# A hand-fixed TensorE order in the experts' stage, and the crowded-expert loop ahead of the first pair

## The chip, the cores and the metric

The kernel runs on one core of a Trainium2 chip. The metric is the device time of one execution in microseconds (us), as the median of several runs. A core has five engines that run their own instruction streams: TensorE (PE in the profile; its weight loads are PEld), VectorE (DVE), ScalarE (ACT), GpSimd (POOL) and SyncE (SP), which here does nothing but issue DMA transfers. They wait for each other by semaphores.

## What is computed

Two model blocks on 256 tokens of width 1024, all in fp32. The change lies in the mixture of experts that ends the first block. The router gives every token two of 32 experts; only the chosen pairs need to be computed:

```python
def hier_moe(h, w_rg, b_rg, w_re, b_re, w_eg, w_eu, w_ed):
    ...
    eid = g_idx * EXP_PER_GROUP + top_i
    gates = jnp.sum(jax.nn.one_hot(eid, N_EXPERTS, dtype=jnp.float32) * (pg_sel * pw)[..., None], axis=1)
    out = jnp.zeros_like(t)
    for e in range(N_EXPERTS):
        hid = jax.nn.silu(t @ w_eg[e]) * (t @ w_eu[e])
        out = out + gates[:, e:e + 1] * (hid @ w_ed[e])
    return out.reshape(bsz, s, d)
```

`w_eg` and `w_eu` are 1024x512 for each expert, `w_ed` is 512x1024. The second block (two hybrid layers) follows; it starts with a norm of the sum of the first block's stream and the experts' output.

## The kernel before

**Places and pairs.** Each expert gets 64 places. Two experts form a pair, so that a pair fills 128 partitions of PSUM, and there are 16 pairs `i`. A product of one expert has 64 weight columns (`z` = 0 or 1, the expert in the pair) and writes the upper or the lower 64 partitions. In the trace an fp32 product is two records: TensorE goes over its data twice.

**The steps of a pair.**
- `gather`: for two pairs at a time, the tokens are picked into their places by products with a 0/1 matrix `sel` (made by VectorE in `select`). The rows stand split in two parts, `h2h` and `h2l`. There are four PSUM banks, `k` = 0, 2, 4, 6; VectorE (k = 0, 4) and ScalarE (k = 2, 6) copy them to `XT`, which has one buffer.
- `front` with `w_eg` (result `pg`), then `front` with `w_eu` (`pu`): 8 values of `k`, two experts, 16 products each.
- `hidden`: tanh on ScalarE, then two passes on VectorE give `hid`.
- `middle`: four transposes of `hid` (`turn`), two of `sel` (`places`), and the gate of each place (`pgs`, two tiny products); ScalarE copies the transposes to `hidT` and `selT`.
- `down`: 16 products with `w_ed`, result `ys` in two banks `n`.
- `scatter`: for each half `n`, `yh` (ScalarE) and `yl` (VectorE), then four products with `selT` into PSUM tiles `mx` (two buffers), which VectorE adds to `x`.

In iteration `i` the program writes `front(pg)`, `middle` of pair i-1, `scatter` of pair i-2, `front(pu)`, `hidden`, sometimes `gather`, and `down` of pair i-1. This is not the order on TensorE: a list scheduler orders each engine's instructions by its own costs and priorities.

**The weights.** They come in 192 loads of 1 MB (two halves for each of 96 matrices; two experts, so four loads for a `front` or a `down`) through one queue of SP, in the order of use (`expert_halves`, L923). The loads go round 18 slots: `wq` (8), `wp` (4) and `wr` (6). From load 162 on, `wp` is left out, since the next layer's weights go there, and 14 slots remain. SP issues a load when the slot's last reader on TensorE is done. Loads use eight semaphores in turn, so that a load also waits for the one eight before it.

**The crowded-expert loop.** `more_rounds` handles experts with more than 64 tokens: every engine reads `mxi` (L1091), the number of further rounds, and branches (L1092). With these inputs it is zero and the body is skipped. An engine that skips it still raises the semaphores which the body would have raised. It does so only when its own work ahead of the branch is done: TensorE's products for TensorE, and all eight load semaphores for SP. The loop stands behind the first pair's `down`.

Of the kernel before, what the change touches and what calls it, by code (L numbers as in the profile page):

```python
# [10 lines left out]
F32 = mybir.dt.float32  # L11
# [8 lines left out]
P = 128  # L20
S = 256
NT = S // P
# [70 lines left out]
class K:  # L93
# [837 lines left out]
    def moe(self, x, es, e0):  # L931
# [19 lines left out]

        def gather(sel, n, XT, first=False):

            def add(ps, k, j, t, hp, start, stop, **kw):
                return nc.tensor.matmul(ps[:, j, :n], hp[:, t, (k + j) * P:(k + j + 1) * P],
                                        sel[:, t].rearrange("p e s -> p (e s)"), start=start, stop=stop, **kw)

            banks = []
            if first:

                for ps, k in zip(self.accT() + self.accT(), range(0, 8, 2)):
                    banks.append(ps)
                    for hp in (h2h, h2l):
                        for j in range(2):
                            ins = add(ps, k, j, 0, hp, hp is h2h and j == 0, False, skip_group_check=True)
                            if hp is h2h and j == 0:
                                head = ins
                            elif hp is h2h:
                                tc.add_manual_dep(ins.ins, head.ins.name, mybir.DependencyInfo(
                                    mybir.DependencyClass.NoSync, mybir.DependencyReason.DATA))  # L970
            for k in range(0, 8, 2):
                ps = banks[k // 2] if first else self.mx.tile([P, 2, 256], F32, name="mx")
                for j in range(2):
                    if first:
                        for hp in (h2h, h2l):
                            add(ps, k, j, 1, hp, False, hp is h2l, skip_group_check=True)
                    else:
                        for i, (hp, t) in enumerate(((h2h, 0), (h2h, 1), (h2l, 0), (h2l, 1))):
                            add(ps, k, j, t, hp, i == 0, i == 3)
                if k % 4:  # L980
                    for j in range(2):
                        nc.scalar.activation(XT[:, k + j, :n], ps[:, j, :n], AF.Copy, scale=self.g2[:, k + j:k + j + 1])
                else:
                    nc.vector.tensor_tensor(XT[:, k:k + 2, :n], ps[:, :, :n],
                                            self.g2[:, k:k + 2].unsqueeze(2).to_broadcast([P, 2, n]), op=ALU.mult)

# [12 lines left out]
        def turn(hid, rows, f=""):  # L999
            hT = q.tile([P, 4, P], F32, name=f + "hidT", tag="XT" if f else "hidT", bufs=1)  # L1000
# [25 lines left out]
        def scatter(sT, py, rows, gs, po=None):  # L1026

            for n in range(2):
                yh, yl = parts(py, n, rows, gs)
                for t in range(NT):  # L1030
                    ps = po[t][n] if po else self.mx.tile([P, 512], F32, name="mx")
                    nc.tensor.matmul(ps, sT[:rows, t], yh[:rows], start=not po, stop=False)
                    nc.tensor.matmul(ps, sT[:rows, t], yl[:rows], start=False, stop=not po)
                    if not po:
                        xs = x[:, t, n * 512:(n + 1) * 512]
                        nc.vector.tensor_add(xs, xs, ps)
# [14 lines left out]

        def front(ps, XT, i):

            o = 2 * (i % 2)
            ww = self.experts()
            for k in range(8):
                for z in range(2):
                    nc.tensor.matmul(ps[64 * z:64 * z + 64], XT[:, k, 64 * (o + z):64 * (o + z + 1)], ww[z][k],  # L1058
                                     start=k == 0, stop=k == 7)
            self.expert_halves(4)  # L1060

        def middle(i, hid, sel):
# [5 lines left out]
            pgs = self.mx.tile([P, 512], F32, name="mx")  # L1068
# [8 lines left out]
        def down(hT):  # L1077
# [3 lines left out]
            for k, n in kn:  # L1081
                for z in range(2):
                    nc.tensor.matmul(py[n][64 * z:64 * z + 64], hT[:, k, 64 * z:64 * z + 64],  # L1083
                                     ww[z][k][:, n * 512:(n + 1) * 512], start=k == 0, stop=k == 3)
            self.expert_halves(4)
            return py

        def more_rounds():
# [3 lines left out]
            with tc.If(n > 0), tc.For_i(0, n, 1):  # L1092
                nc.vector.tensor_scalar(Rm, Rm, -64.0, None, op0=ALU.add)
                with tc.For_i(0, 32, 1) as e:
# [5 lines left out]
                    sel = select(Rc, 0, 1, q, "sel")  # L1100
                    XT = q.tile([P, 8, 64], F32, name="f_XT", tag="XT", bufs=1)
                    gather(sel, 64, XT)
# [20 lines left out]
                    scatter(places(sel[:, :, 0], 64, "f_"), py, 64, gs)  # L1123

        def group(g):

            sels[g] = select(R, 4 * g, 4, p if g % 2 else q, "sel")
            XT = q.tile([P, 8, S], F32, name="XT", bufs=1)
            gather(sels[g], 256, XT, g == 0)
            return XT  # L1130
# [18 lines left out]
        XT = group(0)  # L1149
        G, mxi = self.route_rest(p)  # L1150
        self.out("G", G)

        for i in range(16):
            pg, pu = self.accs(2, 0)
            front(pg, XT, i)
            if i and i != 2:
                mid[i - 1] = middle(i - 1, hid[i - 1], sels[(i - 1) // 2])
            if i > 1:
                scatter(mid[i - 2][1], ys[i - 2], P, mid[i - 2][2])
            front(pu, XT, i)  # L1160
            hid[i] = hidden(pg, pu, P)
            if i == 2 and "positions_2" in A:
                with tc.issue_after(self.hid_ins.ins):
                    self.rope_tables(q)
            if i == 12:
# [3 lines left out]
                for z, g in enumerate(gs2):  # L1169
                    nc.gpsimd.dma_start(self.grow[8 * z:8 * z + 8], g.rearrange("(a b) -> a b", a=8))  # L1170
            if i == 13:
                gsq = factors()
            if i == 1:
                ys[0] = down(mid[0][0])
                mid[1] = middle(1, hid[1], sels[0])
                if self.rounds:
                    more_rounds()
            if i % 2 and i < 15:
                XT = group(i // 2 + 1)
            if i > 1:  # L1180
                ys[i - 1] = down(mid[i - 1][0])
# [5 lines left out]
        scatter(mid[14][1], ys[14], P, mid[14][2], po)  # L1187
        with tc.high_priority(offset=5000):
            ys[15] = down(mid[15][0])
# [844 lines left out]
```

## Time and profile before

| | us |
|---|---|
| median of 3 runs (1845.67 to 1847.8) | 1845.88 |
| profiled execution | 1852.19 |
| its span, first to last instruction | 1850.4 |
| experts' products begin | 183.25 |
| last product of the experts' stage, start of what follows | 688.31 |

The experts' stage so takes 505 us of the span. TensorE is busy for 1771.3 us of the span (96%), VectorE for 977.8 (53%), ScalarE for 743.0 (40%), GpSimd for 117.1 (6%). In the page's 40 slices of 46.3 us each, the DMA rate is 386 and 289 GB/s in the slices from 185 to 278 us, 419 or 420 in the six slices after, then 290, 389 and 166. The page's busy TensorE includes modelled ends and pipelined matmuls, so 96% busy is not 96% at its peak.

### The profile page before, as it was taken

The numbers are of one execution on the slowest core, as the hardware profiler recorded it, in microseconds if no ns is written. First come the engines' busy times: TensorE is split into PE (matmuls) and PEld (weight loads), VectorE is DVE, ScalarE is ACT, GpSimd is POOL, SyncE is SP. The second block draws the span as 40 slices with busy tenths as digits, with TensorE's granted clock in tenths as the row PEclk, the third lists the DMA queues.
The fourth block names the chain that finished last, engine by engine and source line by source line (L and its number), as shares of the span: only waits on it lengthen the run. The fifth ranks groups of instructions, "written<-read, shape, count | busy, mean of one in ns | idle before, by whom it ended". The sixth has DMA issues, their size and how long they took to land. (4 is left out here: it accounts for less than half of the span.)

```text
span 1850.4 us, 27201 instructions
## 1 busy us (share of the span) xinstructions
PE 1771.3 (96%) x10929; PEld 1341.2 (72%) x10929; DVE 977.8 (53%) x1860; ACT 743.0 (40%) x1260; POOL 117.1 (6%) x159
## 2 busy tenths in 40 slices
PE   7999779999999998999999999999999999999998
PEld 6876334433333336879987999997879998999997
DVE  6666022212221227766467585557766567576555
ACT  3454011111111123556464454444555555555443
POOL 4101000000000003000002000002100001100000
PEclk8888989999999999999999999999999999999999
DMA  7456979999997946325644565654414744455552
GB/s 255 148 201 277 386 289 420 419 419 420 419 420 290 389 166 217 108 78 183 194 138 149 185 228 182 188 198 149 163 47 138 217 160 141 147 181 184 192 193 80
DMA packets 153465, 414.51 MB, mean 224 GB/s; under 512 B 13347, under 2 KB 42868, under 8 KB 128632
## 3 DMA queue, kind: packets, MB, share of 16 engines
q1 hardware_dynamic: 152408, 410.49, 62.0%
q0 software_dynamic: 784, 2.18, 0.3%
q8 instruction: 87, 1.43, 0.3%
q14 instruction: 42, 0.34, 0.1%
q10 hardware_dynamic: 144, 0.07, 0.0%
HBM read 411.63 MB, written 2.12 MB: 224 GB/s over the span
## 5 line engine op out<-in xcount | busy, mean ns | idle before, releaser
L170 DVE TENSOR_TENSOR wlo<-raw,whi 128x1024 fp32r<-128x1024 f32 (+4 forms) x372 | 440.2, 1184 | 306.4 <-ACT whi L169 305.7
L169 ACT CAST whi<-raw 128x1024 fp32r<-128x1024 f32 (+4 forms) x384 | 385.4, 1005 | 384.6 <-PE acc L231 155.2
L231 PE MATMUL acc<-xTl,whi 128*128 128x256 f32 x992 | 286.6, 291 | 1.0 <-DVE xTl L385 1.0
L231 PE MATMUL acc<-xTh,whi 128*128 128x256 f32 x992 | 286.7, 291 | 0.0
L231 PE MATMUL acc<-xTh,wlo 128*128 128x256 f32 x992 | 280.4, 290 | 0.0
L1058 PE MATMUL acc<-raw,XT 128*64 128x512 f32 x1024 | 253.0, 605 | 0.0
L231 PEld LDWEIGHTS acc<-xTh,whi 128*128 128x128 f32 x992 | 193.6, 195 | 6.5 <-issue 5.9
L231 PEld LDWEIGHTS acc<-xTl,whi 128*128 128x128 f32 x992 | 193.4, 195 | 6.6 <-issue 5.0
L231 PEld LDWEIGHTS acc<-xTh,wlo 128*128 128x128 f32 x992 | 190.0, 195 | 5.5 <-issue 5.2
L1058 PEld LDWEIGHTS acc<-raw,XT 128*64 128x64 f32 x1024 | 76.4, 139 | 146.9 <-issue 142.3
L1083 PE MATMUL acc<-raw,hidT 128*64 128x512 f32 x512 | 133.6, 597 | 0.0
L178 PE MATMUL acc<-wlo,xTh 128*128 128x512 f32 (+4 forms) x368 | 129.5, 352 | 0.0
L177 PE MATMUL acc<-whi,xTh 128*128 128x512 f32 (+4 forms) x368 | 129.4, 352 | 0.0
L179 PE MATMUL acc<-whi,xTl 128*128 128x512 f32 (+4 forms) x368 | 128.5, 349 | 0.0
L177 PE MATMUL acc<-whi,ffh 128*128 128x512 f32 x256 | 101.0, 394 | 0.0
L178 PE MATMUL acc<-wlo,ffh 128*128 128x512 f32 x256 | 100.7, 393 | 0.0
L179 PE MATMUL acc<-whi,ffl 128*128 128x512 f32 x256 | 100.7, 393 | 0.0
L1083 PEld LDWEIGHTS acc<-raw,hidT 128*64 128x64 f32 x512 | 43.9, 136 | 67.0 <-issue 64.4
L1022 DVE SCALAR_TENSOR_TENSOR yl<-acc,gs,yh 128x512 fp32r<-128x512 f32 x32 | 24.0, 749 | 113.0 <-ACT yh L1021 111.8
L178 PEld LDWEIGHTS acc<-wlo,xTh 128*128 128x128 f32 x368 | 69.6, 189 | 8.4 <-issue 2.2
L177 PEld LDWEIGHTS acc<-whi,xTh 128*128 128x128 f32 x368 | 69.6, 189 | 7.5 <-issue 1.2
L179 PEld LDWEIGHTS acc<-whi,xTl 128*128 128x128 f32 x368 | 69.4, 188 | 7.2 <-issue 1.2
(688 smaller groups left out, 3099.0 us busy)
## 6 DMA issues: line engine op xcount, KB each, us to landing
raw<-in_w_in SPq DMA_DIRECT2D x70, 1024.0 KB, 5.1
raw<-in_w_eg SPq DMA_DIRECT2D x64, 1024.0 KB, 16.6
raw<-in_w_eu SPq DMA_DIRECT2D x64, 1024.0 KB, 17.9
raw<-in_w_ed SPq DMA_DIRECT2D x64, 1024.0 KB, 13.8
raw<-in_w_ff SPq DMA_DIRECT2D x64, 1024.0 KB, 5.2
raw<-in_w_out SPq DMA_DIRECT2D x12, 1024.0 KB
raw<-in_w_branch SPq DMA_DIRECT2D x12, 1024.0 KB, 5.2
raw<-in_w_in SPq DMA_DIRECT2D x8, 792.0 KB
```

The source lines that it names most:

```text
L169: nc.scalar.copy(hi[:, :nk, :n], src)
L170: ins = (nc.gpsimd if pool else nc.vector).tensor_sub(lo[:, :nk, :n], src, hi[:, :nk, :n])
L177: mm(ps, ahi, bhi, start=start, stop=False)
L178: mm(ps, ahi, blo, start=False, stop=False)
L179: self.mm_ins = mm(ps, alo, bhi, start=False, stop=stop)
L231: ins = mm(ps[c // 2][:, c % 2, :], w[:, j, c * P:(c + 1) * P], x[:, kx + k + j, :], start=first and c % 2 == 0, stop=k + j == nk - 1 and ...
L1022: nc.vector.scalar_tensor_tensor(yl[:rows], py[n][:rows], gs, yh[:rows].bitcast(F32), op0=ALU.mult, op1=ALU.subtract)
L1058: nc.tensor.matmul(ps[64 * z:64 * z + 64], XT[:, k, 64 * (o + z):64 * (o + z + 1)], ww[z][k], start=k == 0, stop=k == 7)
L1083: nc.tensor.matmul(py[n][64 * z:64 * z + 64], hT[:, k, 64 * z:64 * z + 64], ww[z][k][:, n * 512:(n + 1) * 512], start=k == 0, stop=k == 3)
```

## The change

1. `manual_schedule` for TensorE: from the first iteration on, its instructions run in the order in which the program writes them. The other engines are scheduled as before.
2. The program writes them so that the products of the two experts with the same `k` (and `n`) always follow each other. `middle` of pair i-1 comes behind `k` = 1 of `front(pg)`, the scatter of half 0 behind `k` = 4, half 1 behind `k` = 0 of `front(pu)`. In odd iterations the banks of `gather` come behind `k` = 5 and 6 of `front(pu)` and behind the second and fourth step of `down`. `down` of pair i-1 comes after `hidden` in every iteration, also for i = 1.
3. `pgs` takes a `tp` tile in place of an `mx` tile. `tp` has two buffers and now gets three tiles in each `middle`.
4. `more_rounds` comes before the first pair. Its tiles have tags that fit there.

```diff
-        def scatter(sT, py, rows, gs, po=None):
+        def scatter(sT, py, rows, gs, n, po=None):
...
-        def front(ps, XT, i):
+        def front(ps, XT, i, between={}):
...
+                if k in between:
+                    between[k]()
             self.expert_halves(4)
...
-            pgs = self.mx.tile([P, 512], F32, name="mx")
+            pgs = self.tp.tile([P, 512], F32, name="tp")
...
-        XT = group(0)
+        sels[0] = select(R, 0, 4, q, "sel")
+        XT = q.tile([P, 8, S], F32, name="XT", bufs=1)
+        gather(sels[0], 256, XT)
         G, mxi = self.route_rest(p)
         self.out("G", G)
-
+        if self.rounds:
+            more_rounds()
+
+        es.enter_context(tc.manual_schedule(engines={mybir.EngineType.PE}))
         for i in range(16):
+            def turn_last(i=i):
+                mid[i - 1] = middle(i - 1, hid[i - 1], sels[(i - 1) // 2])
+            spread = lambda n, i=i: scatter(mid[i - 2][1], ys[i - 2], P, mid[i - 2][2], n)
             pg, pu = self.accs(2, 0)
-            front(pg, XT, i)
-            if i and i != 2:
-                mid[i - 1] = middle(i - 1, hid[i - 1], sels[(i - 1) // 2])
-            if i > 1:
-                scatter(mid[i - 2][1], ys[i - 2], P, mid[i - 2][2])
-            front(pu, XT, i)
+            front(pg, XT, i, {1: turn_last if i else lambda: None,
+                              4: (lambda: spread(0)) if i > 1 else lambda: None})
+            group, banks = i % 2 and i < 15, {}
...
+            front(pu, XT, i, {0: (lambda: spread(1)) if i > 1 else lambda: None,
+                              5: lambda: take(0), 6: lambda: take(2)})
             hid[i] = hidden(pg, pu, P)
+            if group:
+                XT = q.tile([P, 8, S], F32, name="XT", bufs=1)
+                put(0), put(2)
...
+            if i:
+                ys[i - 1] = down(mid[i - 1][0], {1: lambda: put(4), 3: lambda: put(6)})
...
-            if i == 1:
-                ys[0] = down(mid[0][0])
-                mid[1] = middle(1, hid[1], sels[0])
-                if self.rounds:
-                    more_rounds()
-            if i % 2 and i < 15:
-                XT = group(i // 2 + 1)
-            if i > 1:
-                ys[i - 1] = down(mid[i - 1][0])
```

**TensorE around the branch.** Before, the read of `mxi` stands behind the first pair's `down` (L1083), with the second pair's transposes (L1003, L1011) between:

```order
L1083 MATMUL acc_1940<-raw,hidT 64x512 x4
L1083 MATMUL acc_1941<-raw,hidT 64x512 x4
L1003 MATMUL tp<-const,hid 128x128 x4
L1011 MATMUL tp<-const,sel 128x128 x2
L1091 TENSOR_LOAD mxi
```

Now it stands behind the first gather (L956), and the first pair's products (L1066) come behind the branch:

```order
L956 MATMUL acc_1749<-sel,h2h 128x256
L956 MATMUL acc_1749<-sel,h2l 128x256
L956 MATMUL acc_1749<-sel,h2h 128x256
L956 MATMUL acc_1749<-sel,h2l 128x256
L1103 TENSOR_LOAD mxi
```

What moved past it: four `front` groups, the `down` of the first pair and the `middle` of two pairs.

**SP around the branch.** Before, 38 loads of experts' weights stand ahead of the read of `mxi`; the last of them are:

```order
L923 DMA raw<-in_w_eu 128x2048 x4
L923 DMA raw<-in_w_ed 128x2048 x4
L923 DMA raw<-in_w_eg 128x2048 x4
L923 DMA raw<-in_w_eu 128x2048 x2
L1091 TENSOR_LOAD mxi
```

Now it is 18, as many as there are slots:

```order
L923 DMA raw<-in_w_eu 128x2048 x4
L923 DMA raw<-in_w_eg 128x2048 x4
L923 DMA raw<-in_w_eu 128x2048 x4
L923 DMA raw<-in_w_ed 128x2048 x2
L1103 TENSOR_LOAD mxi
```

So 20 loads moved from ahead of the branch to behind it.

**TensorE in the middle of the stage.** Before, where a pair begins (a raw tile stands for one half of one expert's matrix; 2754 and 2827 belong to expert 0 of the pair, 2756 and 2829 to expert 1). These rows are about 384.5 to 396 us of the trace:

```order
L1058 MATMUL acc0_2958<-raw_2754,XT_2766 64x512
L1032 MATMUL mx_3018<-yh_3014,selT_2871 128x512
L1032 MATMUL mx_3022<-yh_3014,selT_2871 128x512
...
L1058 MATMUL acc0_2958<-raw_2756,XT_2766 64x512
...
L1058 MATMUL acc0_2958<-raw_2827,XT_2766 64x512
L955 MATMUL mx_3059<-sel_3055,h2l_1515 128x256
L955 MATMUL mx_3069<-sel_3055,h2h_1514 128x256 x2
...
L1058 MATMUL acc0_2958<-raw_2829,XT_2766 64x512
```

Now, where a pair begins (L1012, L1020 and L1080 are `middle`; 4 products of L1066 are two `k` of both experts):

```order
L1066 MATMUL acc_2228<-raw,XT 64x512 x4
L1012 MATMUL tp<-const,hid 128x128 x4
L1020 MATMUL tp<-const,sel 128x128 x2
L1080 MATMUL tp<-G,sel 128x2 x2
L1066 MATMUL acc_2228<-raw,XT 64x512 x6
L1040 MATMUL mx<-yh,selT 128x512
L1041 MATMUL mx<-yl,selT 128x512
L1040 MATMUL mx<-yh,selT 128x512
L1041 MATMUL mx<-yl,selT 128x512
L1066 MATMUL acc_2228<-raw,XT 64x512 x6
```

The scatter and gather products stood between the two experts of one `k`; now only whole `k` steps are parted. The number of products is the same in both.

## Rows read from the trace of the kernel before

**Rows 1.** Stretches of the span: start:end, then busy time by engine, clock, DMA.

```profile
core 0: us, PE busy (x) PEld busy (x) DVE busy (x) ACT busy (x) POOL busy (x), PEclk, DMA share, GB/s
177.00:186.00 9.00, 8.44 (x61) 6.53 (x62) 5.23 (x29) 1.88 (x5) 0.00 (x0) 1.00 0.00 1
222.00:239.00 17.00, 0.56 (x5) 0.35 (x3) 0.00 (x0) 0.51 (x1) 0.00 (x0) 0.58 0.99 408
239.00:253.00 14.00, 10.60 (x44) 5.77 (x46) 2.79 (x4) 2.32 (x6) 0.00 (x0) 0.66 0.11 24
253.00:583.00 330.00, 320.63 (x1437) 129.40 (x1433) 81.70 (x152) 43.27 (x81) 0.00 (x0) 0.99 1.01 418
...
666.00:688.00 22.00, 21.82 (x84) 8.85 (x82) 3.27 (x5) 4.60 (x9) 0.00 (x0) 1.00 0.04 7
```

**Rows 2.** TensorE in time order: start, length, records, idle time before and its releaser.

```profile
220.40 0.51 PE L955 MATMUL mx<-sel,h2h 128*128 128x256 f32 x2 [0.83 <-ACTq L1092]
220.75 0.40 PE L955 MATMUL mx<-sel,h2l 128*128 128x256 f32 x2
220.98 0.40 PE L955 MATMUL mx<-sel,h2h 128*128 128x256 f32 x2
...
242.40 0.79 PE L955 MATMUL mx<-sel,h2h 128*128 128x256 f32 x2 [19.85 <-DVE XT L984]
...
246.11 8.23 PE L1058 MATMUL acc<-raw,XT 128*64 128x512 f32 x32
```

**Rows 3.** The branch's instructions: count, duration (ns, three times), first and last start.

```profile
L1091 POOLq TENSOR_LOAD <-mxi x1: 500/500/500, 180.3 to 180.3; - x1
...
L1092 SPq EVENT_SEMAPHORE  x8: 17/17/17, 223.1 to 240.8; - x8
...
L1092 PEldq COMPARE_BRANCH  x1: 3125/3125/3125, 215.8 to 215.8; - x1
```

**Rows 4.** Waits between 200 and 262 us: waiter, awaited, us, times, longest.

```profile
ACT yh L1021 <- SPq L1092: 18.2, 1, 18.2
```

**Rows 5.** SP's load issues in time order: start, length until the last one's issue.

```profile
163.77 1.00 SPq L923 DMA_DIRECT2D raw<-in_w_ed  x2
...
186.93 1.38 SPq L923 DMA_DIRECT2D raw<-in_w_ed  x2
...
344.28 9.44 SPq L923 DMA_DIRECT2D raw<-in_w_eg  x4
...
558.34 7.92 SPq L923 DMA_DIRECT2D raw<-in_w_eg  x4
```

**Rows 6.** TensorE in time order, products of the experts and what parts them.

```profile
183.25 20.82 PE L1058 MATMUL acc<-raw,XT 128*64 128x512 f32 x96
...
393.64 1.07 PE L1058 MATMUL acc<-raw,XT 128*64 128x512 f32 x2
394.65 0.39 PE L955 MATMUL mx<-sel,h2l 128*128 128x256 f32 x1
...
395.91 10.08 PE L1058 MATMUL acc<-raw,XT 128*64 128x512 f32 x45
```

**Rows 7.** TensorE's waits for other engines, 250 to 689 us.

```profile
PE mx L955 <- ACT XT L982: 3.7, 4, 0.9
...
PE mx L1033 <- DVE yl L1022: 0.2, 1, 0.2
```

**Rows 8.** A `middle` in the timeline: TensorE's first transposes, and ScalarE's copy of them.

```profile
218.69 0.66 PE L1003 MATMUL tp<-const,hid 128*128 128x128 f32 x4
```

```profile
219.44 0.59 ACT L1004 COPY hidT<-tp 128x512 f32<-128x512 f32 x1 [13.88 <-PE tp L1003]
```

**Rows 9.** DMA issues of the page: count, size, median us from issue to landing.

```profile
raw<-in_w_in SPq DMA_DIRECT2D x70, 1024.0 KB, 5.1
```

**Rows 10.** A stretch in which TensorE's granted clock (third number from the end) falls.

```profile
574.00:580.00 6.00, 5.45 (x18) 2.24 (x20) 1.28 (x2) 0.00 (x0) 0.00 (x0) 0.72 1.02 425
```

**Rows 11.** The end of the stage: the first record behind it.

```profile
688.31 2.05 PE L306 MATMUL tp<-grow,const 8*128 8x128 f32 x16
```

More of the change, by code (lines that the diff above doesn't have):

```diff
@@ L950, in select, with gather @@
             return sel
-        def gather(sel, n, XT, first=False):
+        def gather(sel, n, XT=None):
             def add(ps, k, j, t, hp, start, stop, **kw):
@@ L956, in add, with bank, turned @@
                                         sel[:, t].rearrange("p e s -> p (e s)"), start=start, stop=stop, **kw)
[L958 to L972, printed above, removed]
-                for j in range(2):
[L974 to L979, printed above, removed]
+            def bank(k, ps=None):
+                if ps is None:
+                    ps = self.mx.tile([P, 2, 256], F32, name="mx")
+                    parts = ((h2h, 0), (h2h, 1), (h2l, 0), (h2l, 1))
+                else:
+                    parts = ((h2h, 1), (h2l, 1))
+                for j in range(2):
+                    for i, (hp, t) in enumerate(parts):
+                        add(ps, k, j, t, hp, len(parts) == 4 and i == 0, i == len(parts) - 1,
+                            skip_group_check=len(parts) == 2)
+                return ps
+            def turned(k, ps, XT):
                 if k % 4:
@@ L985, in gather @@
                                             self.g2[:, k:k + 2].unsqueeze(2).to_broadcast([P, 2, n]), op=ALU.mult)
+            if XT is None:
+                return bank, turned
+            banks = self.accT() + self.accT()
+            for ps, k in zip(banks, range(0, 8, 2)):
+                for hp in (h2h, h2l):
+                    for j in range(2):
+                        ins = add(ps, k, j, 0, hp, hp is h2h and j == 0, False, skip_group_check=True)
+                        if hp is h2h and j == 0:
+                            head = ins
+                        elif hp is h2h:
+                            tc.add_manual_dep(ins.ins, head.ins.name, mybir.DependencyInfo(
+                                mybir.DependencyClass.NoSync, mybir.DependencyReason.DATA))
+            for ps, k in zip(banks, range(0, 8, 2)):
+                turned(k, bank(k, ps), XT)
         def hidden(pg, pu, rows, f=""):
@@ L999, in turn @@
         def turn(hid, rows, f=""):
-            hT = q.tile([P, 4, P], F32, name=f + "hidT", tag="XT" if f else "hidT", bufs=1)
+            hT = q.tile([P, 4, P], F32, name=f + "hidT", tag="hidT", bufs=1)
             pt = self.tp.tile([P, 4, P], F32, name="tp")
@@ L1024, in parts @@
             return yh, yl
-        def scatter(sT, py, rows, gs, po=None):
[L1028 to L1036, printed above, removed]
+        def scatter(sT, py, rows, gs, n, po=None):
+            yh, yl = parts(py, n, rows, gs)
+            for t in range(NT):
+                ps = po[t][n] if po else self.mx.tile([P, 512], F32, name="mx")
+                nc.tensor.matmul(ps, sT[:rows, t], yh[:rows], start=not po, stop=False)
+                nc.tensor.matmul(ps, sT[:rows, t], yl[:rows], start=False, stop=not po)
+                if not po:
+                    xs = x[:, t, n * 512:(n + 1) * 512]
+                    nc.vector.tensor_add(xs, xs, ps)
         def scatter_last(sT, py, gs, po):
@@ L1075, in middle, with down @@
             return hT, sT, gs
-        def down(hT):
+        def down(hT, between={}):
             py = self.accs(2, 1)
@@ L1080, in down @@
             kn = (0, 0), (1, 0), (0, 1), (1, 1), (2, 0), (3, 0), (2, 1), (3, 1)
-            for k, n in kn:
+            for m, (k, n) in enumerate(kn):
                 for z in range(2):
@@ L1084, in down @@
                                      ww[z][k][:, n * 512:(n + 1) * 512], start=k == 0, stop=k == 3)
+                if m in between:
+                    between[m]()
             self.expert_halves(4)
@@ L1099, in more_rounds @@
                     nc.vector.tensor_copy(Gc, G[:, :, one])
-                    sel = select(Rc, 0, 1, q, "sel")
-                    XT = q.tile([P, 8, 64], F32, name="f_XT", tag="XT", bufs=1)
-                    gather(sel, 64, XT)
+                    sel = select(Rc, 0, 1, q, "f_sel")
+                    XT = p.tile([P, 8, 64], F32, name="f_XT", tag="sel", bufs=1)
+                    bank, turned = gather(sel, 64)
+                    for k in range(0, 8, 2):
+                        turned(k, bank(k), XT)
                     pg, pu = self.accs(2, 0)
@@ L1122, in more_rounds @@
                             nc.tensor.matmul(py[n2][0:64], hT[:, k, 0:64], c, start=k == 0, stop=k == 3)
[L1123 to L1130, printed above, removed]
+                    sT = places(sel[:, :, 0], 64, "f_")
+                    for n2 in range(2):
+                        scatter(sT, py, 64, gs, n2)
         def factors():
@@ L1186, in moe @@
                 nc.tensor.matmul(po[t][n], self.ident, x[:, t, n * 512:(n + 1) * 512], start=True, stop=False)
-        scatter(mid[14][1], ys[14], P, mid[14][2], po)
         with tc.high_priority(offset=5000):
-            ys[15] = down(mid[15][0])
+            ys[15] = down(mid[15][0], {2 * n + 2: lambda n=n: scatter(mid[14][1], ys[14], P, mid[14][2], n, po)
+                                       for n in range(2)})
             scatter_last(mid[15][1], ys[15], mid[15][2], po)
```

5 lines of the change are left out of this document (added).

## The prediction

> **What bounds the kernel now.** I read the clock and the stretches first, then TensorE's own time line, then SP's issues. In the long middle of the stage, 253 to 583 us, TensorE is busy for 320.6 of 330 us at a granted clock of 0.99, and the 16 DMA engines are busy for all of it at 418 GB/s [rows 1]. So two limits lie close together, and both have to be priced.
>
> *TensorE's:* SP's group of issues at 344.28 and the one at 558.34 lie 84 loads apart, that is seven pairs: 214.06 / 7 = 30.58 us a pair [rows 5]. *The loads':* a load is 1024 KB, 1.0486 MB, which at 418 GB/s takes 2.51 us; twelve a pair make 30.1 us. TensorE is the later one, by half a microsecond a pair, so whatever is saved on TensorE alone soon meets the loads.
>
> Outside this middle there are two holes. One is at the branch: from 222 to 239 TensorE does 0.56 us of work, and then from 239 to 253 the DMA share is 0.11 [rows 1]. The other is ahead of the stage: all 18 slots are filled by loads issued up to 164.8, the queue is empty from 177 to 186, and the next load goes out at 186.93, 3.7 us after the first product at 183.25 [rows 1, 5, 6]. The stage ends at 688.31 [rows 11].
>
> **The branch: what goes.** SP at the branch waits for every load in flight; its eight waits last from 223.1 to 240.8 [rows 3]. ScalarE's `yh` stands behind them for 18.2 us [rows 4], and TensorE waits 19.85 us at 242.40 for `XT`, in the middle of a gather [rows 2]. Since SP can issue nothing, the DMA hole follows. Without the branch there, TensorE is free at 220.40 - 0.83 = 219.57. A gather is 32 products; two of them start 0.23 apart [rows 2], so 0.115 each, 3.7 in all, and 0.3 for the return to the experts' products: 223.6. They came at 246.11, 22.5 later. The third of a `front` pair that follows took 8.23 us for 32 records; at the rate of 96 records in 20.82 [rows 2, 6] it is 6.94, and the 1.3 between is the clock of 0.66 that the hole left behind [rows 1]. Removed: **23.8 us**.
>
> **The branch: what it costs at its new place.** SP's eight waits now meet only the first 18 loads, and the queue is at rest from 177 on [rows 1], so they cost nothing; GpSimd's read of `mxi` at 180.3 shows that the number is there before the first product at 183.25 [rows 3, 6]. TensorE's own compare and branch took 3.1 us [rows 3], then in the shade of work already queued; now the gather ahead of it is short (3.7 us, with waits for copies). The bounds are 0.3 (it all lies in the shade) and 6 (3.1 twice, since read, branch and semaphore hand-over come one after the other with empty queues). I take half of 3.1 and a little, **1.75**: the gather hides the read, not all of the branch. First product at S = 185. Queued behind it are all experts' products and SP's 19th load; that load waits for TensorE anyway. Net for the branch: -22.0.
>
> **The splits.** Two neighbouring products on the upper and the lower 64 partitions run side by side: 96 records in 20.82 us are 48 products, 24 side-by-side steps of 0.867 us [rows 6]. A lone product takes the whole step: the one at 393.64 is followed by the next work at 394.65, 1.01 later, against 0.867 [rows 6]. Going through the two orders and counting a step for each pair and for each lone product, before needs 418 steps for 384 pairs of products, and after 384. **34 x 0.867 = 29.5 us** go, all of it on TensorE's path.
>
> **The returns.** Going from products to other work and back costs 1.01 - 0.867 = 0.14 out, and 395.91 - 394.65 = 1.26 for nine records of 0.115 (1.03) or so, 0.2 back [rows 6]. The orders have 64 returns before and 76 after: 12 x 0.34 = **+4.1 us**.
> The Trainium skill, "TensorEngine Tiling (Array Packing)", section Key Properties, says that changing the tiling mode drains the TensorE, and gives no figure; it speaks against the twelve more, the trace agrees that a return is not free, and by the rows' 0.34 it is the 4.1 above.
>
> **The waits.** In 250 to 689 us TensorE's waits for other engines make nine rows, from 3.7 us to 0.2, and 12.8 us together [rows 7]. They belong to the old order and go with it: -12.8. The new order has one wait that I can see: the `pgs` tile is the third `tp` of a `middle` and `tp` has two, so that it waits for ScalarE's copy of the first. The transposes began at 218.69 and the copy ended at 219.44 + 0.59 = 220.03 [rows 8], 1.34 later, when the six transposes (6 x 0.115 = 0.69) are long done: 0.65 a pair, x16 = **+10.4**. Nothing lies in front of it but the transposes, so nothing hides it, and all products behind it wait. Elsewhere I followed who makes what each instruction waits for: `hid` is done some products earlier, `yh` and `yl` a whole `front` earlier, the adds of `x` free `mx` before the next half. As bounds, 5 (ScalarE gets to the copy sooner at full clock) and 35 (10.4 and another 1.5 a pair, TensorE at the mercy of ScalarE and VectorE in their own orders).
>
> **Sum on TensorE.** -22.0 - 29.5 + 4.1 - 12.8 + 10.4 = -49.8: the stage ends at 688.3 - 49.8 = 638.5.
>
> **Sum of the loads.** The 19th load goes at S + 3.7 = 188.7; a load without a queue takes 5.1 us to land [rows 9], 2.5 of it transfer, so the stream starts at 191.3. The 174 loads after the first 18 take 174 x 2.51 = 436.7: the last lands at 628.0. Behind it stand four steps (3.5) and the last scatter (eight products of 512 columns, twice 0.115 each, 1.9, and some 1 for `yh` and `yl`): 634.4. So the loads allow 634, TensorE 638.5, and TensorE stays the later by a hair; with (638.5 - 185) / 16 = 28.3 us a pair it eats up the 18 loads it has in store (16 x 1.8 = 29 us of their 45). The 22 us of DMA rest before 688 (share 0.04, [rows 1]) go for the most part; the next stage's loads that stand behind the last expert's are hidden by TensorE's last steps: three by 2.51 reach 635.5, before 638.5.
>
> **To the median.** The trace is of an execution of 1852.2 us, 6.3 above the median of 1845.9; I take the gain off both: 1802.4 for such an execution, **1796** for the median.
>
> **Rivals.**
> *Stalls of the fixed order.* The scheduler could put other work in front of a late operand; the fixed order waits. Four gather banks, two scatter halves and a `middle` a pair each hang on a copy by VectorE or ScalarE. For it: the nine waits exist even in the scheduled order, the largest at the gather's banks behind ScalarE's copy to `XT` [rows 7]. Against it: each block has at least one product step of 0.867 us on either side, and the copies take some 0.6 [rows 8]. With 1 to 2 us a pair, 16 to 32 us come back: 1812 to 1828. Chance 0.14.
>
> *The clock (slower).* Where TensorE paused between small blocks at 574 to 580, its granted clock was 0.72 [rows 10], between the levels of 1.2 and 2.4 GHz: a fall costs 6 x 0.28 = 1.7 us. The new order has three interruptions a pair with a wait in one of them. 49.8 / 1.7 = 29 falls, about two a pair, eat up the gain; three a pair, 48, cost 82 and give 1878. Against it: in 330 us of such interruptions the mean clock is 0.99 [rows 1], 3.3 us lost, that is two falls. Chance 0.04.
> The Trainium skill, "TensorE: Matmul & The Clock Gate", section "A second HAM failure mode: psum-queue depth-cycling", tells of a kernel whose short idles between groups of matmuls made the clock swing; it would give this rival's time, and the 0.99 here speaks against it.
>
> *The branch doesn't get free.* If a load or a late `mxi` holds the engines at the new place, some 10 us of the 22 come back, 1806. Against it: the rest of the queue from 177 [rows 1]. Chance 0.05.
>
> *The loads rule.* If they move at 410 GB/s, not 418, the last lands 8.5 later, the stage ends at 643 and the time is 1800. Chance 0.05, inside the forecast's range.
>
> **How the numbers follow.** The forecast has 0.72, together with the loads' rival the stretch from 1788 to 1806. Its lower end: S at 183.6 and the loads as the only limit, 633, 1790.6, less 2 or 3 since the next stage's loads come earlier too. The upper end takes in most of the stalls: 1824. The stalls' worse part, the clock and lucky ends stay out, under 2 in 10. About 0.2% (3.7 us) is what a measurement here can tell from no change. Faster by more: 0.72 + 0.14 + 0.05 + 0.05 = 0.96, less 0.02 for stalls and falls of the clock that together eat up just the gain, which are the chance of the same; slower 0.04 (the clock).
>
> **What would show it.** *Branch:* no TensorE wait of 20 us, no DMA hole at 239, first product at 184 to 187. *Splits:* no experts' product alone; steps of 0.867 throughout. *Waits:* a row of TensorE waiting for ScalarE's `hidT`, about 0.65 x 16; other rows together a few us. *Loads:* 418 GB/s from about 191 to 628, with the wait for a load not among TensorE's larger ones until the end. *End:* the first record behind the stage near 638. The prediction is wrong if TensorE waits for loads from the middle on, if the granted clock in the stage is under 0.97, or if rows of waits for VectorE or ScalarE make up over 25 us.

## The result and the profile after

The changed kernel takes 1803.2 us (median of 4 runs, 1797.9 to 1806.6) against 1846.8 of the kernel before: ratio 0.976, 95% interval 0.973 to 0.979. Run again with the experiments, it took 1800.7 against 1849.1, ratio 0.974 (0.972 to 0.977). The forecast was 1796, range 1788 to 1824.

All kernels of this study run the same code up to the stage and after it, but the stage's begin drifts: the first experts' product starts at 180.2 us in one run and at 185.6 in another, also between two runs of the changed kernel (184.7 and 183.2). What follows the stage takes 1161 to 1164 us in every trace. So the traces are compared by the **stage time**, from the first experts' product to the `L306` record behind the stage: 688.31 - 183.25 = 505.1 us before [rows 6, 11], 639.00 - 184.73 = 454.3 after. The gain is 50.8 us in the stage, 48.6 in the span (1850.4 to 1801.8). A stage time is that of one trace; the two traces of the changed kernel differ by 1.0 us (454.3 and 455.3).

TensorE in the trace of the changed kernel: start, length, records, idle time and releaser. These rows answer to [rows 2, 6 and 11]:

```profile
183.53 0.28 PE L956 MATMUL acc<-sel,h2l 128*128 128x256 f32 x1
184.73 15.67 PE L1066 MATMUL acc<-raw,XT 128*64 128x512 f32 x72 [0.92 <-DVEq L1104]
...
522.61 4.46 PE L1093 MATMUL acc<-raw,hidT 128*64 128x512 f32 x18
528.07 3.22 PE L1093 MATMUL acc<-raw,hidT 128*64 128x512 f32 x13 [1.01 <-DMA raw<-in_w_ed]
...
533.06 1.93 PE L1066 MATMUL acc<-raw,XT 128*64 128x512 f32 x6 [1.34 <-DMA raw<-in_w_eg]
...
618.08 3.65 PE L1093 MATMUL acc<-raw,hidT 128*64 128x512 f32 x14 [0.67 <-DMA raw<-in_w_ed]
...
639.00 2.05 PE L306 MATMUL tp<-grow,const 8*128 8x128 f32 x16
```

The branch now costs one idle stretch of 0.92 us, and the wait of 19.85 is gone. The stage ends at 639.0. New are three waits for loads, at 528, 533 and 618.

TensorE's waits in the stage of the changed kernel (waiter, awaited, us in all, times, longest), which answer to [rows 7]:

```profile
PE tp L1080 <- ACT hidT L1013: 8.0, 16, 0.5
PE acc L1093 <- DMA raw<-in_w_ed: 1.7, 2, 1.0
PE acc L1066 <- DMA raw<-in_w_eg: 1.3, 1, 1.3
PE acc L1066 <- DVEq L1104: 0.9, 1, 0.9
PE tp L306 <- ACT raw L1151: 0.3, 1, 0.3
```

None of the nine rows of before is left; the 0.3 us at `L306` is for another copy than before. Stretches of the changed kernel's span, with the columns of [rows 1]:

```profile
230.00:500.00 270.00, 265.39 (x1263) 106.23 (x1263) 71.54 (x135) 36.52 (x68) 0.00 (x0) 1.00 1.01 420
500.00:560.00 60.00, 56.63 (x268) 23.51 (x266) 14.23 (x24) 7.34 (x14) 0.00 (x0) 1.00 1.01 420
560.00:590.00 30.00, 29.43 (x143) 13.12 (x144) 7.50 (x12) 5.82 (x11) 0.00 (x0) 0.94 1.01 420
...
610.00:630.00 20.00, 18.82 (x79) 7.71 (x76) 2.88 (x5) 2.19 (x4) 0.00 (x0) 1.00 1.01 411
```

The loads run at 420 GB/s without the hole that stood at 239. TensorE's own pace, in two pairs with one gather, is from one `middle` to the next but one, **55.58 us** in place of the 61.16 (2 x 30.58) of before:

```profile
308.98 0.66 PE L1012 MATMUL tp<-const,hid 128*128 128x128 f32 x4
...
364.56 0.66 PE L1012 MATMUL tp<-const,hid 128*128 128x128 f32 x4
```

The loads of two pairs need 24 x 2.497 = 59.9 us (1.0486 MB at 420 GB/s). So now TensorE is the faster by 2.2 us a pair and eats its store of loaded weights. Near 523 the store is empty.

### The profile page after: what moved, and what is told of

It reads as the page before. It is cut to its first block, busy times and chain, and to the rows that moved or that the text cites. A ratio compares the mean times of both kernels' runs of the same rounds, so it can differ in the third digit from the quotient of the medians.

```text
span 1801.8 us, 27176 instructions
## 1 busy us (share of the span) xinstructions
PE 1743.4 (97%) x10929; PEld 1334.0 (74%) x10929; DVE 978.7 (54%) x1860; ACT 743.3 (41%) x1260; POOL 116.5 (6%) x159
## 5 line engine op out<-in xcount | busy, mean ns | idle before, releaser
L1066 PE MATMUL acc<-raw,XT 128*64 128x512 f32 x1024 | 237.0, 600 | 2.3 <-DMA raw<-in_w_eg 1.3
L1066 PEld LDWEIGHTS acc<-raw,XT 128*64 128x64 f32 x1024 | 69.8, 137 | 126.7 <-issue 118.9
L1093 PE MATMUL acc<-raw,hidT 128*64 128x512 f32 x512 | 118.3, 596 | 1.7 <-DMA raw<-in_w_ed 1.7
L1093 PEld LDWEIGHTS acc<-raw,hidT 128*64 128x64 f32 x512 | 37.2, 137 | 68.3 <-issue 60.6
L1030 ACT ACTIVATE yh<-acc,gs 128x512 fp32r<-128x512 f32 x32 | 22.0, 687 | 136.8 <-PE acc L1093 136.8
## 6 DMA issues: line engine op xcount, KB each, us to landing
raw<-in_w_eg SPq DMA_DIRECT2D x64, 1024.0 KB, 19.9
raw<-in_w_eu SPq DMA_DIRECT2D x64, 1024.0 KB, 19.9
raw<-in_w_ed SPq DMA_DIRECT2D x64, 1024.0 KB, 19.9
```

Source lines behind the costliest of these rows:

```text
L1030: nc.scalar.activation(yh[:rows], py[n][:rows], AF.Copy, scale=gs)
```

## The experiments

| kernel | median us | ratio to before (95%) | stage us |
|---|---|---|---|
| before | 1846.8 | 1 | 505.1 |
| changed | 1803.2 | 0.976 (0.973 to 0.979) | 454.3 |
| changed, again | 1800.7 | 0.974 (0.972 to 0.977) | 455.3 |
| branch first, old order | 1833.5 | 0.991 (0.989 to 0.993) | 485.4 |
| new order, branch at its old place | 1809.5 | 0.978 (0.976 to 0.980) | 463.1 |
| some interruptions inside a step | 1819.6 | 0.984 (0.982 to 0.985) | 472.5 |
| all interruptions inside a step | 1801.6 | 0.975 (0.973 to 0.976) | 455.8 |
| 16 loads fewer | 1799.2 | 0.973 (0.971 to 0.975) | 449.1 |
| gate in the bank of `places` | 1804.2 | 0.976 (0.974 to 0.977) | 455.3 |
| the same, 16 loads fewer | 1804.8 | 0.975 (0.973 to 0.977) | 458.1 |
| gate in an `mx` bank | 1799.0 | 0.973 (0.971 to 0.975) | 453.6 |
| the same, 16 loads fewer | 1784.8 | 0.966 (0.963 to 0.968) | 436.9 |
| gate in `mx`, last `middle` earlier | 1797.5 | 0.972 (0.970 to 0.975) | 452.6 |
| no branch (one run) | 1800.2 | | 454.4 |

Each ratio is to the runs of before on the same chip (medians 1846.8 to 1850.4).

### Each half of the change alone

The loop ahead of the first pair, with the order left to the scheduler:

```diff
         self.out("G", G)
+        if self.rounds:
+            more_rounds()
...
-                if self.rounds:
-                    more_rounds()
```

> The kernel before, with its own scheduled order; only the crowded-expert loop is moved ahead of the first pair. Theory (TensorE is the later limit, terms add up): the branch gives its 22.0 us; the scheduler's new order has 421 steps of products in place of 418 and 68 returns in place of 64, which takes 2.6 + 1.4 back: 18 us less than before, about 1828, and the stage ends near 670 in place of 688. Rival (the hole at the branch was rest that the loads needed anyway, and the gain is all of the order): within 4 us of before. The trace should show no wait of 20 us on TensorE and no DMA hole at 239 by the one, the same rest spread over the stage by the other.

Measured: 16 us less in the median (1833.5 for 1849.7), 505.1 to 485.4 in the stage, 19.7 less. TensorE behind the second pair's transposes, in this kernel's trace:

```profile
219.83 0.66 PE L1003 MATMUL tp<-const,hid 128*128 128x128 f32 x4
...
225.11 7.09 PE L1058 MATMUL acc<-raw,XT 128*64 128x512 f32 x32
```

From the transposes to the next experts' products it is now 5.3 us. Before it was 246.11 - 218.69 = 27.4 [rows 2, 8], and the products then took 8.23 for 7.09: 22.1 + 1.1 = 23.2 went, where 23.8 was forecast. The theory holds, with the scheduler's own extra steps.

The other half, the new order with the loop behind the first pair's `down`:

```diff
-        if self.rounds:
-            more_rounds()
...
+            if i == 1:
+                mid[1] = middle(1, hid[1], sels[0])
+                if self.rounds:
+                    more_rounds()
```

> The changed kernel with the loop back behind the first pair's down (38 loads ahead of the branch, as before). Theory: the order alone is worth 29.5 (splits) - 4.1 (returns) + 12.8 - 8.0 (waits, with the 8.0 that the changed kernel's trace shows for hidT) = 30 us, less nothing for the loads, since behind the hole at the branch the last load could still land near 640: about 1816, 12 to 22 us above the changed kernel. Rival (each part alone gives most, since the loads are the true limit): 1805 to 1809. Rival (the branch at its old place costs more under a fixed order, because nothing can be taken ahead of the wait): 1825 or more.

Measured: 1809.5, stage 463.1, only 8.9 above the changed kernel. This is a miss: neither the theory's 12 to 22 nor its 30 us for the order. The number is next to that of the loads' rival, but in this trace TensorE waits for no load, so that rival does not explain it. The branch is there in full, as TensorE and two stretches show:

```profile
228.50 6.21 PE L1066 MATMUL acc<-raw,XT 128*64 128x512 f32 x20 [1.34 <-DVEq L1104]
241.98 0.79 PE L1040 MATMUL mx<-yh,selT 128*128 128x512 f32 x1 [7.26 <-ACT yh L1030]
```

```profile
230.00:240.00 10.00, 4.71 (x16) 1.15 (x12) 0.00 (x0) 0.00 (x0) 0.00 (x0) 0.84 0.91 372
240.00:245.00 5.00, 3.02 (x6) 1.41 (x8) 2.65 (x4) 1.27 (x2) 0.00 (x0) 0.50 0.44 149
```

SP's eight waits and their branch:

```profile
L1104 SPq EVENT_SEMAPHORE  x8: 17/17/17, 227.2 to 241.1; - x8
```

SP is through at 241.1, where it was 240.8 before [rows 3]. But in the fixed order the gather lies ahead of the branch, so that TensorE gets past it at 228.5 and not at 220.4 [rows 2], and behind it stand five product steps (to 234.7) that need nothing of ScalarE or SP. TensorE works while SP waits: its wait is 7.3 in place of 19.9. SP issues the next load at 241.58, where before it was 250.93, and the DMA share from 239 to 253, 0.11 before [rows 1], is 0.68.

What this costs TensorE is read from the first product to the third pair's `middle`, here and in the kernel with 16 loads fewer (below), which has the same order and no wait for a load; their first products stand at 183.56 and 180.24:

```profile
264.79 0.66 PE L1012 MATMUL tp<-const,hid 128*128 128x128 f32 x4
```

```profile
248.90 0.66 PE L1012 MATMUL tp<-const,hid 128*128 128x128 f32 x4
```

That is 81.2 for 68.7, 12.6 us. (Over the whole stage it is 463.1 for 449.1, 14.0; the clock behind 560, 0.91 for 0.96, can make the rest.) So one branch at one place has two prices: about 23 us in the old order, and some 13 in the new one, of which the loads' waits of the changed kernel hide 5. The two halves give 19.7 and 42.0 alone, and 50.8 together.

### What a lone product costs

In some interruptions (half 0 of the scatter, the gather's first and third bank) the block is written between the two experts of a step:

```diff
-                if k in between:
-                    between[k]()
+                    if k in between and z == (k not in (4, 5)):
+                        between[k]()
```

> The changed kernel with the scatter of half 0 (k = 4), the first gather bank (k = 5) and the third (second step of down) put between the two experts of a step, the other interruptions left between steps. Counted from the order: 412 steps of products, 28 more, as many returns as before. Theory (a lone product costs a whole step of 0.867): TensorE has 24.3 more; the 3.0 us that it now waits for loads take up 3 of it: 21 us above the changed kernel, about 1824. Rival (a lone product costs half a step, and the split order's price was in the waits): 8 to 12 us above. Rival (nothing): within 3 us.

Then in all of them (`z == 0`):

> The changed kernel with every interruption in front and down put between the two experts of a step. No interruption leaves the two experts of its step adjacent, but between two interruptions the products of the two experts still alternate, so that the second expert of one step can run beside the first of the next: counted so, 387 steps, 3 more than in the changed kernel. Theory (what counts is that neighbours lie on opposite halves, not that they are one step): within 3 us of the changed kernel, about 1803. Rival (only the two products of one step run side by side, or a broken step costs a lone one): 73 broken steps, 60 us, about 1860.

Measured: 472.5, 18.2 more, and 455.8, half a microsecond more than the changed kernel's second run. A scatter in the changed kernel, and then in the kernel with some interruptions inside a step:

```profile
396.83 2.80 PE L1066 MATMUL acc<-raw,XT 128*64 128x512 f32 x12
...
400.68 3.65 PE L1066 MATMUL acc<-raw,XT 128*64 128x512 f32 x16
```

```profile
373.27 2.79 PE L1066 MATMUL acc<-raw,XT 128*64 128x512 f32 x10
...
377.11 4.50 PE L1066 MATMUL acc<-raw,XT 128*64 128x512 f32 x18
```

Ten records (five products) take as long as twelve, and eighteen as long as twenty, which the changed kernel shows elsewhere:

```profile
486.20 4.51 PE L1066 MATMUL acc<-raw,XT 128*64 128x512 f32 x20
```

So the product that is left over takes a whole step, 0.85 us. In two pairs four steps are added, and their time, `middle` to `middle` as above, goes from 55.58 to 59.0: 3.42 / 4 = 0.855. With some interruptions inside a step, and then with all:

```profile
227.29 0.65 PE L1012 MATMUL tp<-const,hid 128*128 128x128 f32 x4
...
286.29 0.65 PE L1012 MATMUL tp<-const,hid 128*128 128x128 f32 x4
```

```profile
224.50 0.65 PE L1012 MATMUL tp<-const,hid 128*128 128x128 f32 x4
...
280.23 0.66 PE L1012 MATMUL tp<-const,hid 128*128 128x128 f32 x4
```

With some of them the stage grew by 18.2, less than 28 x 0.855 = 23.9, because the changed kernel's waits for loads went: to the 449.1 that TensorE needs without them (below), 23.9 make 473.0.

With every interruption inside a step, two pairs take 55.73, only 0.15 more than in the changed kernel. This pace is free of the loads, which hide a little of the stage time in both. By the count, 3 products in the stage are left over; all others pair, the second expert of one step with the first of the next one. So what counts is not that the two experts of a `k` stand together, but that an even number, alternating between the halves, stands between two interruptions. By the count, the old order lacked that 34 times.

### Which limit sets the end

Sixteen loads less for the queue: four pairs' products of `w_eu` read the `w_eg` tiles again (`w1`).

```diff
+        k.skip = 3, 6, 9, 12
+        k.order = [o for o in k.order if o[1] != 1 or o[0] not in k.skip]
...
-            front(pu, XT, i, {...})
+            front(pu, XT, i, {...}, w1 if i in self.skip else None)
```

The changed kernel again, as the mark, and this one:

> The changed kernel once more, as the mark for the three runs beside it: 454.3 us from the first experts' product to the record behind the stage, and TensorE's waits for loads near 523 to 530 and 618, as in its first trace.

> The changed kernel, leaving out 16 of the 192 loads: in four pairs the products of w_eu read the w_eg tiles again, so the work of every engine but the queue is the same and only what those four pairs compute is not the model's. 16 loads are 40 us of the queue. Theory (TensorE's own path would end some 4 us ahead of the loads, which set the end of the changed kernel): its waits for loads vanish, the stage takes 450 us in place of 454.3, about 4 us less. Rival (TensorE sets the end, as was forecast, and the few waits for loads are swallowed by later ones): within 1 us. Rival (the queue sets the pace of the whole stage): 20 to 40 us less.

The mark took 455.3. With fewer loads TensorE waits for no load at all, and the stage takes 449.1 (180.24 to 629.35), as the theory said, 5.2 and 6.2 less than in the two traces of the changed kernel. (The medians, 1799.2 and 1800.7, do not tell them apart, so that this rests on the traces.) Where the loads hold TensorE is seen at the same `middle`, in the first trace of the changed kernel and with fewer loads:

```profile
534.92 0.66 PE L1012 MATMUL tp<-const,hid 128*128 128x128 f32 x4
```

```profile
526.81 0.66 PE L1012 MATMUL tp<-const,hid 128*128 128x128 f32 x4
```

Up to it the first product lies 350.2 and 346.6 back: 3.6 of the 5.2 come from the waits at 528 and 533. The other 1.5 come behind it, where the one wait at 618 stands. In the second trace of the changed kernel TensorE waits for no load behind 533, and of its 6.2 the delay up to this `middle` makes 3.4; the rest goes with a lower clock from 560 to 600, 0.87 for 0.96.

So the loads cost 5.2 in the first trace, more than the 3.0 of the waiting rows. A likely reason, not tried by itself: a wait for one expert's half leaves the other expert's product alone, and what that loses is in no row.

Then the wait for `hidT` was taken away, first by writing the gates into the free part of the bank of `places`:

```diff
-            sT = places(selw, P)
-            pgs = self.tp.tile([P, 512], F32, name="tp")
+            sT, pgs = places(selw, P, gate=True)
```

> The changed kernel with the gate products written into a free quarter of the bank of the places' transposes, so that no third tile is taken and TensorE does not wait for ScalarE's copy (8.0 us in 16 waits). Theory (the loads set the end): the 8.0 go from that row and come back as waits for loads; the stage stays within 1.5 us of 454.3. Rival (TensorE sets the end): 446, 8 us less.

> Both edits at once: 16 loads fewer (the same four pairs read w_eg tiles again) and the gate products in the places' bank. Theory (loads and TensorE are two limits of which the later one counts): with the loads out of the way the 8.0 us show: the stage takes 442, 12 us less than the changed kernel, 8 less than with fewer loads alone. Rival (the 8.0 us are hidden by something else than the loads): as with fewer loads alone.

Neither tells the theories apart, since the wait did not go. The first one's waits and a `middle`:

```profile
PE tp L1079 <- ACT selT L1023: 12.6, 16, 0.8
```

```profile
255.07 0.38 PE L1020 MATMUL tp<-const,sel 128*128 128x128 f32 x2
256.24 0.61 PE L1079 MATMUL tp<-G,sel 128*128 128x2 f32 x4 [0.79 <-ACT selT L1023]
```

The gate products now wait until ScalarE has read the other part of the same bank, 0.79 in place of 0.51. With fewer loads that gave 458.1, not 442: 449.1 plus 4.2 for the longer waits (12.4 for 8.2), and the 4.8 that are left are about what the clock takes, 0.83 in 560 to 600 us in place of 0.96, 40 x 0.13 = 5.2.

So the gates went back to an `mx` bank, as before the change:

```diff
-            pgs = self.tp.tile([P, 512], F32, name="tp")
+            pgs = self.mx.tile([P, 512], F32, name="mx")
```

> The changed kernel with the gate products back in an mx bank, as in the kernel before, so that neither ScalarE's copy of hidT nor that of selT is waited for; the mx banks' last readers are then long done. Theory (the loads set the end): the 8.0 us of hidT waits go, waits for loads take their place, and the stage stays within 1.5 us of the 454.3 and 455.3 of the two runs of the changed kernel. Rival (TensorE sets the end): 446 to 447.

> 16 loads fewer (four pairs read the w_eg tiles again in place of w_eu) and the gate products in an mx bank. Theory (with the loads out of the way TensorE's path counts in full): 449.1 of the run with fewer loads, less the 8.2 of its hidT waits: 441. Rival (the waits were covered by something else): 448 to 450.

Measured: 453.6, as the theory said, and 436.9 with fewer loads, where the medians tell it too (1784.8 for 1799.2). With the loads out of the way the wait is worth 449.1 - 436.9 = 12.2 us, 0.76 a pair, more than the 0.51 of its row: without it the gate products also overlap the end of the transposes, and the next products start sooner behind them. With all loads it is worth 0.7 to 1.7: it comes back as waits for loads, 6.9 us in six, three near 461 to 472 and three near 521 to 532:

```profile
461.65 3.65 PE L1093 MATMUL acc<-raw,hidT 128*64 128x512 f32 x16 [0.77 <-DMA raw<-in_w_ed]
466.64 3.22 PE L1093 MATMUL acc<-raw,hidT 128*64 128x512 f32 x13 [1.34 <-DMA raw<-in_w_ed]
...
531.58 1.93 PE L1066 MATMUL acc<-raw,XT 128*64 128x512 f32 x6 [1.33 <-DMA raw<-in_w_eg]
...
636.95 2.04 PE L306 MATMUL tp<-grow,const 8*128 8x128 f32 x16
```

So with all loads in place they take most of what TensorE saves by this edit. Whether it is the last loads that count was tried by moving the last `middle`, and two of four copies of `x`, ahead of the last loads' arrival:

```diff
+                ys[i - 1] = down(mid[i - 1][0], {...} if i < 15 else {3: early, 5: early_x})
...
-        mid[15] = middle(15, hid[15], sels[7])
```

> The changed kernel with the gate products in an mx bank and less work behind the load that comes last but four: the last middle goes between the two halves of the down of pair 14, where TensorE waits for loads, and two of the four copies of x (those that go to mx banks) behind its sixth step. Theory (the loads set the end, and the end is the landing of the last but four plus the 21 us of TensorE's work behind it): 1.9 of middle and 1.7 of copies go from those 21, the stage takes about 451, 3 to 4 less than the changed kernel. Rival (TensorE sets the end): as with the gate products in an mx bank alone, since no work is left out.

Measured: 452.6, 1.0 less than without the move, and the clock in 560 to 600 was 0.91 for 0.87, 40 x 0.04 = 1.6, which is worth no less. So the theory fell for this kernel and its rival stands: in this trace and in the one above, TensorE waits for no load behind 533. In both it is the loads up to 533 that count, not the last. Behind that point TensorE has more to do per load again (a gather, 32 records of `L306` with a fall of the clock, the copies of `x`, the last scatters), and its own work sets the end. For the changed kernel itself the move was not tried, and its first trace, where the clock fell less (0.96), has a wait at 618 once more. Which load is the last to hold TensorE so differs from execution to execution.

Last, the changed kernel without the branch:

> The changed kernel without the crowded-expert loop and its branch (with these inputs the loop has no rounds). The forecast put the branch at its new place at 1.75 us. Theory: the 1.2 us between the last gather product's start and the first experts' product shrinks to 0.3 or so, where only XT is waited for, 0.9 us in all, too little for the time to tell. Rival (the branch holds more than the trace of TensorE shows): the stage gets shorter by 3 us or more.

```profile
181.97 5.37 PE L1066 MATMUL acc<-raw,XT 128*64 128x512 f32 x24 [0.32 <-DVE XT L977]
```

An idle time of 0.32 in place of 0.92, and a stage of 454.4: the branch at its new place costs 0.6 us.

## Why the prediction was right, and where it was so by luck

**The branch: right, but not as a price of its own.** 23.2 us went in the old order, 23.8 were forecast. Its new place was put at 1.75 and costs 0.6; of TensorE's 3.1 us for compare and branch [rows 3] the changed trace shows 0.37:

```profile
L1104 SPq EVENT_SEMAPHORE  x8: 17/17/17, 179.9 to 180.4; - x8
...
L1104 PEldq COMPARE_BRANCH  x1: 367/367/367, 180.9 to 180.9; - x1
```

SP's eight waits took 0.5 us, as the empty queue let expect. What the forecast did not say: the 23 us belonged to the branch in the old order. With the new order, the branch at its old place costs some 13 on TensorE's path, and 8.9 in the stage.

**The splits: right.** A step was put at 0.867 and measured at 0.855; the 34 are a count.

**The waits: right in kind.** The nine rows went, and the one wait that was named came, 16 times. Its row shows 8.0, the kernels with fewer loads 12.2, and 10.4 was forecast. No other wait of the fixed order appeared, so that the rival of stalls fell.

**The returns** (4.1 us) were not tried alone.

**The sum on TensorE was 4 us too high.** 638.5 - 185 = 453.5 was forecast for TensorE alone; the kernel with fewer loads shows 449.1. Which term holds the 4.4 is open. A part can be the clock, for which the sum has no term: 0.83 from 570 to 590 before, 3.4 us, and some 1.8 with fewer loads. And the waits of before may have cost more than the 12.8 of their rows, as that for `hidT` did.

**The loads: right in their sum, wrong in the floor.** The last load was issued at 608.1 and landed some 20 us later, 628, the 628.0 of the forecast:

```profile
L923 SPq DMA_DIRECT2D raw<-in_w_ed x64: 327/328/551, 162.6 to 608.1; - x64
...
DMA to landing us min/median/max: 7.5/19.9/20.7
```

But the forecast laid a floor under the last load alone (634.4). In the trace of the changed kernel the tightest floor is the load four before it:

```profile
597.91 0.33 SPq L923 DMA_DIRECT2D raw<-in_w_ed  x1
```

It landed 19.9 later, at 617.8; TensorE waited for it until 618.08 and then needed 20.9 to the end, 639.0. By the forecast's own numbers this floor was 628.0 - 4 x 2.51 + 20.9 = 638.9. The loads awaited until 533 lay another: 534.92, and 102.5 from that `middle` to the end with fewer loads (526.81 to 629.35), 637.5. TensorE's own path would have ended at 184.7 + 449.1 = 633.8. So "TensorE stays the later by a hair" was wrong, and so was the sign that it named, no larger waits for loads until the end.

The store was taken as 45 us of loads, of which 29 are eaten by the end. But by 522.61 TensorE had used 148 loads in 337.9 us, 2.28 each, where the queue brings one in 2.49: 31 were eaten by then. The 29 came from a mean over the whole stage, and that holds the last 21 us, in which TensorE takes its last loads and then none, so that it is too slow for what lies before. Another 6 or 7 went since the loads' stream starts that much behind the first product (at 191.3 by the forecast), and what is left, some 7, is three loads, of which a step needs two landed before it.

TensorE was 4.4 faster than forecast and the loads held it back by 5.2: so the end fell on 639.0, for 638.5 forecast. That the two errors cancel is luck. Each of the two alone would have missed by some 4 to 5 us, within the range.

**To the median: missed by 7.** The executions with a trace went from 1852.2 to 1803.6, where 1802.4 was forecast. But that of before stood 6.3 above the median of its time and that of the changed kernel 0.4 above its own, so that the same 6.3 taken off both gave 1796 for a median of 1803.2. The medians fell by 43.6, and in the second set by 48.4 (1849.1 to 1800.7), near the 48.6 of the traces.

**The clock: right.** With three interruptions a pair and a wait in one of them, the granted clock stays at 1.00 from 230 to 560. What the Trainium skill tells in "TensorE: Matmul & The Clock Gate", section "A second HAM failure mode: psum-queue depth-cycling", of a clock that swings with short idles between groups of matmuls, did not happen here. Within the stage the clock fell only behind the `L306` records. The stretch that priced this rival, 574 to 580 before [rows 10], has such records too, so its 0.72 is not the price of a pause alone:

```profile
574.26 0.71 PE L306 MATMUL tp<-grow,const 16*128 16x128 f32 x4
```

## What to carry to other kernels

Where two streams race, lay a floor at each point, the arrival of the n-th load plus the other engine's work behind it, and not only at the last load. Price a barrier together with what stands right behind it on the engine that meets it: the same branch cost 23 us before a gather that needed other engines, and some 13 behind the gather and before five steps that needed nothing. When products on two halves of the array run side by side, count that an even number, alternating, stands between two interruptions; whether the interruption parts a logical pair doesn't matter.

## What the runs showed of the hardware

The clock can fall almost without a gap. Near 565 us of the changed kernel stand 32 records of `L306`, products over 8 rows that spread a row of `grow` over the partitions, with 0.27 us of idle time between them:

```profile
563.63 2.05 PE L306 MATMUL tp<-grow,const 8*128 8x128 f32 x16
565.95 2.05 PE L306 MATMUL tp<-grow,const 8*128 8x128 f32 x16 [0.27 <-ACT raw L1151]
```

The granted clock of 560 to 600 is 0.96 in one run of this kernel and 0.87 in the next, 0.83 in the kernel with fewer loads and the gate in the bank of `places`: 40 us x 0.04 to 0.17, 1.6 to 6.8 us, which can be a part of the spread between runs. It does not always fall: with the branch first and the old order, `L306` stands in blocks of 2 to 16 records between other products, and the clock from 540 to 610 is 1.00. That the few rows are the reason was not tried. Three stretches behind 560 us, of the kernel with the last `middle` earlier (columns as in [rows 1]):

```profile
560.00:570.00 10.00, 9.73 (x52) 6.34 (x50) 2.88 (x4) 4.11 (x8) 0.00 (x0) 0.80 1.01 421
570.00:580.00 10.00, 10.00 (x44) 3.88 (x44) 1.60 (x4) 0.86 (x2) 0.00 (x0) 0.86 1.01 417
580.00:590.00 10.00, 10.00 (x46) 3.46 (x44) 3.03 (x4) 0.60 (x1) 0.00 (x0) 1.00 1.01 419
```

And a row of waits can show less than the wait costs: 0.51 for 0.76 behind `hidT`, 3.0 in all for 5.2 behind the loads of the first trace.
